# A feed-forward's operand places, its tanh, the splits at the turn, and the loads of the last unit

## The chip, the cores and the metric

The kernel runs on one core of one Trainium2 chip. The metric is the device time of one execution in microseconds, and less is better. Six engines and queues appear below: PE (TensorE, matmuls), PEld (its weight loads), ACT (ScalarE), DVE (VectorE), POOL (GpSimd), and SP (SyncE), which issues the DMAs here.

## What is computed

One encoder layer over 2048 tokens of width 1024, in fp32: windowed attention and a two-way mLSTM beside each other, an output projection, and then the feed-forward, which is the part in question:

```python
hff = rms_norm(x, g_norm2) * (1.0 + scale2) + shift2
gte, up = jnp.split(hff @ w_ffn_in, 2, axis=-1)       # 1024 -> 2 x 2816
ff = (jax.nn.silu(gte) * up) @ w_ffn_out              # 2816 -> 1024
return x + gate2 * ff                                 # then a final rms_norm
```

## The kernel before

Up to about 1000 us the kernel does attention, mLSTM and the output projection; the change touches nothing of it. The rest is the feed-forward, and each of its two products is one level of Strassen and Winograd: seven products of half size in place of eight. The operands are sums and differences of quarters, named A11, A12, S1 to S4, A22 on one side and B11, B21, B22, T1 to T4 and the like on the other. Each operand is split into two parts, hi (a copy that ScalarE rounds) and lo (the rest, by a subtraction on VectorE, line 1370 for the token side, 1405 for the weights, 1666 and 1675 in the down projection). Each product of operands is three matmuls in `mm3` (lines 56, 57, 58: hi by hi, hi by lo, lo by hi).

**Up projection.** `pair(hh, j)` is a unit: one column tile of gate and up for one half of the tokens. It runs seven products (`prod(0)` to `prod(6)`, 12 matmuls of 128x512 each), and between them the evacuations of PSUM: `s1_`, `g0`, a tanh into `t0` (silu is made from it), `u2`, `c5`, `u3`, a second tanh, and so on; these small tiles come from six buffers in turn (`ot`). There are 44 units, numbered from 0: 22 for the first half of the tokens, then 22 for the second in reversed order. Between unit 21 and unit 22 lies the turn: unit 22 uses the weights of unit 21 again, and `refill_ops(1)` loads the second half's seven operands from `hop_d` and splits them (`finish_op`, two halves of 128x1024 for each). Weights for the next unit are loaded (`load_raw`) and split (`weights`) beside the current one. The split weights are the stationary operands of these matmuls, and go through a ring of twelve tiles: four `big`, four `w`, and r0 to r3 in the pool `ff`.

A unit's results are combined on POOL and stored to `a_d` in DRAM. A store is put on a list and issued at the next unit's start (`stores`, line 1539).

**Down projection.** For each of seven operand kinds it runs over 11 k and 8 blocks of rows, 1848 matmuls in all. The stationary operands are `ah` and `al` (`raw_a` loads them from `a_d`, line 1661; `split_a` splits them), which go through the ring `aring` of eight tiles; `w2` goes through `wring`. The first of these loads and splits begin in the last unit of the up projection.

**What sets the order.** The program is written in one sequence; the build reorders it by priority and free buffers, and then each engine works its own queue strictly in order, and so does SP with its DMAs. A tile is written again only when all readers of its last content are done.

**Places.** Before, r0 to r3 are at bytes 204,768 to 221,152 of each partition and the rows `x1t` and the tiles `xt` in the pool `xp`; the other eight tiles of the weights' ring are below 158,720.

Of the kernel before, what the change touches and what calls it, by code (L numbers as in the profile page):

```python
# [11 lines left out]
F32 = mybir.dt.float32  # L12
# [3 lines left out]
AF = mybir.ActivationFunctionType  # L16
ALU = mybir.AluOpType
MUL, ADD, SUB, MAX, MIN = ALU.mult, ALU.add, ALU.subtract, ALU.max, ALU.min
# [3 lines left out]
P = 128  # L22
T = 2048
D = 1024
# [12 lines left out]
def hybrid_layer_kernel(  # L37
# [93 lines left out]
    def big(i, name, shape=(P, 2, 512), dt=F32R):  # L131

        return hp.tile(list(shape), dt, tag=f"big{i}", name=name)
# [112 lines left out]
    with tc.tile_pool(name="sw", bufs=2, side="right", reuse_waits="tile") as sw:  # L246
# [135 lines left out]
        r = rsqrt(s1, ssq, 4, D, "rs")  # L382
# [928 lines left out]

    def norm2(hh, z, tags, lead):
        n = BO[2 * hh + z]
        xt = [xp.tile([P, D], F32, tag="xt", name="x1t", bufs=4) for _ in range(4)]
        for i in range(4):
            sp.dma_start(xt[i], x1_d[(4 * n + i) * P:(4 * n + i + 1) * P, :])
        op = {o: hop_d[hh, i] for i, o in enumerate(OPS)}
        new = lambda: xp.tile([P, 512], F32, tag="n2", name="n2", bufs=5)
        for _ in range(lead):
            yield True  # L1320
        ssq = xp.tile([P, 4], F32, tag="ssq", name="ssq")
        for i in range(4):
            jk = xp.tile([P, D], BF16, tag="junk", name="junk", bufs=1)
            act.activation(jk, xt[i], AF.Square, accum_out=ssq[:, i:i + 1])
            yield True
        r = rsqrt(xp, ssq, 4, D, "rs")
        yield True
        yield True
        for i in range(4):
            act.activation(xt[i], xt[i], AF.Copy, scale=r[:, i:i + 1])  # L1330
            yield True
        if z == 0:
            for k in range(KT):
                t = new()
                turned(t, xt, k, tags[k % 2], gs2, mod[:, 3, :])
                yield True
                sp.dma_start(op["B11" if k < 4 else "B21"][k % 4], t)
        else:
            for k in range(4):
                b11, b21, b12, b22, t3 = (new() for _ in range(5))  # L1340
                sp.dma_start(b11, op["B11"][k])
                sp.dma_start(b21, op["B21"][k])
                turned(b12, xt, k, tags[0], gs2, mod[:, 3, :])
                yield True
                turned(b22, xt, k + 4, tags[1], gs2, mod[:, 3, :])
                yield True
                dve.tensor_tensor(t3, b22, b12, SUB)
                dve.tensor_tensor(b12, b12, b11, SUB)
                dve.tensor_tensor(b11, b22, b12, SUB)
                yield True  # L1350
                dve.tensor_tensor(b21, b21, b11, SUB)
                for o, t in (("B22", b22), ("T3", t3), ("T1", b12), ("T2", b11)):
                    sp.dma_start(op[o][k], t)
                yield True
                sp.dma_start(op["T4"][k], b21)

    def refill_ops(hh):


        hls = []  # L1360

        def start(u):
            hls.append([[big(4 * u + 2 * z + i, OPS[u]) for i in range(2)] for z in range(2)])
            for i in range(2):
                sp.dma_start(hls[u][1][i].bitcast(F32), hop_d[hh, u, 2 * i:2 * i + 2].rearrange("k p t -> p k t"))

        def finish(u):
            for hi, lo in zip(*hls[u]):
                act.activation(hi, lo.bitcast(F32), AF.Copy)
                dve.tensor_tensor(lo, lo.bitcast(F32), hi.bitcast(F32), SUB)  # L1370

        return hls, finish, start

    ring = deque([("big", f"big{i}") for i in range(28, 32)] + [("w", f"w{i}{z}") for i in (1, 0) for z in "hl"]
                 + [("ff", f"r{i}") for i in range(4)])
    pools = {"w": wp, "big": hp}

    def ring_tile(name, shape=(P, 2, 512)):
# [14 lines left out]
        sp.dma_start(v(a22), w_ffn_in[512:1024, cu].rearrange("(k p) c -> p k c", p=P))  # L1393
        return g, a21, a22

    def weights(raw, early=False):

        g, a21, a22 = raw
        a11, a12 = g[:, :512], g[:, 512:]
        ws_ = {}  # L1400

        def part(n, f):
            t = ws_[n] = ring_tile(n)
            act.activation(t[:, 0, :], f, AF.Copy)  # L1404
            dve.tensor_tensor(t[:, 1, :], f, t[:, 0, :].bitcast(F32), SUB)  # L1405

        f1, f2 = (xd.tile([P, 512], F32, tag="n2", name="sf", bufs=9) if early else
                  pools["ff"].tile([P, 512], F32, tag="sf", name="sf", bufs=2) for _ in range(2))
        pool.tensor_tensor(f1, a21, a22, ADD)  # L1409
        pool.tensor_tensor(f2, f1, a11, SUB)  # L1410
        part("A11", a11)
        yield True
        part("A12", a12)
        pool.tensor_tensor(a21, a11, a21, SUB)
        yield True
        pool.tensor_tensor(a12, a12, f2, SUB)
        part("S2", f2)
        yield True
        part("S1", f1)
        yield True  # L1420
        part("S3", a21)
        yield True
        part("S4", a12)
        yield True
        part("A22", a22)
        yield [ws_[n] for n in ("A11", "A12", "S2", "S1", "S3", "S4", "A22")]

    NPR, KH, raws, put_off = NT // 2, DFF // P // 2, [], []
# [97 lines left out]
    with tc.tile_pool(name="ff", bufs=1, side="right", reuse_waits="tile") as ff:  # L1526
# [15 lines left out]
        def pair(hh, j, ws_, hop, after=lambda u: None, then=lambda u: None):  # L1542
# [20 lines left out]
            then(0)  # L1563
            prod(1, ps2, True)
            dve.tensor_tensor(g0, ps2, s1_, ADD)
            act.activation(t0, g0, AF.Tanh, scale=0.5)
            dve.scalar_tensor_tensor(g0, t0, 1.0, g0, ADD, MUL)
            then(1)
            prod(2, ps1)
            act.activation(u2, ps1, AF.Copy)  # L1570
            then(2)
            prod(3, ps5, True)
            act.activation(c5, ps5, AF.Copy)
# [40 lines left out]
        JO = [m * KH + j for j in range(KH) for m in range(2)]  # L1614
        units = [(0, j) for j in JO] + [(1, j) for j in reversed(JO)]
        wseq = deque(JO[2:] + JO[-2::-1])
        raw, = raws
        for n, (hh, j) in enumerate(units[:-1]):
            ws_, turn = nxt_w, n == NJ - 1
            start = lambda u: None  # L1620
            if turn:
                hop1, finish_op, start = refill_ops(1)
                assert not norms
            else:
                more_w = weights(raw)
            STEPS = (0, 0, 0, 2, 2, 1, 2) if n == 0 else (0, 0, 1, 1, 2, 2, 1)

            def beside(u):

                nonlocal nxt_w, raw  # L1630
                if n == 0 and u < 3:
                    finish_op(u + 4)
                if n == NJ and u < 2:
                    finish_op(u + 5)
                if turn:
                    if u > 1:
                        finish_op(u - 2)
                    return
                for _ in range(STEPS[u]):
                    nxt_w = next(more_w)  # L1640
# [7 lines left out]
                hop = hop1  # L1648


        aring = deque([("ff", f"r{i}") for i in range(4)] + [("w", f"w{i}{z}") for i in (1, 0) for z in "hl"])
        wring = deque([("xp", "xt")] * 4)

        def from_ring(rg, name, shape):
            pl, tag = rg[0]
# [159 lines left out]
        def evac(u, i, ps):  # L1815
            if u == "A11":
                ra.append(big(16 + i, "ra", (P, D), F32))
            if u == "S3":
                rb.append(big(24 + i, "rb", (P, D), F32))
            a, b = (t[i] if i < len(t) else None for t in (ra, rb))  # L1820
            if u in ("A11", "S2", "S3", "A22"):
                z, m = {"A11": (a, 0), "S2": (a, 1), "S3": (b, 1), "A22": (b, 0)}[u]
# [18 lines left out]
        for u in ("A11", "S2", "S3", "A22", "S1", "S4", "A12"):  # L1841
# [17 lines left out]
                if u == "S1" and 0 < k <= 8:  # L1859
                    row0(k - 1)  # L1860
            if u == "A12":
                aring.extendleft(("big", f"big{31 - i}") for i in range(8))
            tail = [operands(u, k) for k in range(KH - KL, KH)]
            for i in range(8):
                for k, (a, w) in enumerate(tail):
# [32 lines left out]
```

## Time and profile before

| | |
|---|---|
| median of 3 runs | 2327.73 us (2326.14 to 2330.36) |
| profiled execution, span | 2327.4 us |
| PE busy | 2247.9 us, 97% of the span |
| DVE, ACT, POOL busy | 1579.2, 1060.3, 1047.7 us |
| units 0 to 20 and 23 to 42 | 19.0 to 20.7 us each |
| unit 21, unit 22 (the turn) | 20.8, 31.2 us |
| unit 43 (the last) | 27.0 us |
| first six k of the down projection | 41.1 us |

Rows of windows give, for each stretch, the busy time of each engine with its count, then the TensorE clock that was granted (1.00 is full), the share of time in which the DMA engines were busy, and GB/s. Rows of the timeline give start, length, engine, line, tile written and read, and in brackets how long the engine had stood idle and what ended that. Rows of waits give line waited at, what was waited for, microseconds in all, times, and the longest.

### The profile page before, as it was taken

Reading aid. Unit: us, or ns where it says so; the run is one execution under the profiler, and the core shown is the slowest. Engines: PE = TensorE matmul, PEld = TensorE weight load, DVE = VectorE, ACT = ScalarE, POOL = GpSimd, SP = SyncE. Lnnn points to the kernel's source line nnn. Section 1 sums busy time; section 2 is a strip of 40 time slices with the busy share of each in tenths; the row PEclk is TensorE's granted clock in tenths of the full one; section 3 lists DMA queues with packets and bytes.
Section 4 is the critical chain, followed back from the end, with each engine's and each line's share of the span. In section 5 each row is a group of like instructions: output and inputs, shape, how many; then the busy total and the mean of one; then the engine's idle time right before and its main releaser. Section 6 shows DMA issues by size and latency. Waiting matters only on the chain.

```text
span 2327.4 us, 32438 instructions
## 1 busy us (share of the span) xinstructions
PE 2247.9 (97%) x10822; PEld 1864.0 (80%) x10822; DVE 1579.2 (68%) x2931; ACT 1060.3 (46%) x2206; POOL 1047.7 (45%) x876
## 2 busy tenths in 40 slices
PE   7999999999999999999999999899999989999998
PEld 4997778888788878778888887788788868888887
DVE  6786567656787797786656767666666636684594
ACT  5423555544677655344444434333333323232352
POOL 1006534334334344536565665556565643592020
PEclk9999999999999999999999999999999989999999
DMA  8486755686756667754343545223232373442462
GB/s 329 153 251 211 241 169 158 187 235 173 214 173 190 182 225 244 236 208 145 109 168 104 172 150 217 68 95 109 95 109 95 126 259 104 162 151 99 135 218 91
DMA packets 355499, 393.38 MB, mean 169 GB/s; under 512 B 21388, under 2 KB 253180, under 8 KB 355332
## 3 DMA queue, kind: packets, MB, share of 16 engines
q1 hardware_dynamic: 355108, 391.28, 52.0%
q8 instruction: 85, 1.39, 0.2%
q14 instruction: 82, 0.67, 0.1%
q10 hardware_dynamic: 224, 0.04, 0.0%
HBM read 272.05 MB, written 119.19 MB: 168 GB/s over the span
## 4 chain that ended last, share of the span: by engine, by line
PE 53%; DMA 2%; DVE 2%; issue 1%; ACT 1%; POOL 0%; SPq 0%; ACTq 0%; DVEq 0%; POOLq 0%
PE fp L56 11%; PE fp L57 11%; PE fp L58 11%; PE fo L58 6%; PE fo L57 6%; PE fo L56 6%; DMA a_d<-u 1%; PE ops L56 1%; PE ops L57 1%; PE ops L58 1%; DMA al<-a_d 1%; DVE S L1405 0%; DMA B<-hop_d 0%; PE trn L166 0%; DMA T<-hop_d 0%
## 5 line engine op out<-in xcount | busy, mean ns | idle before, releaser
L466 PE MATMUL gps<-hT,whi 128*128 128x512 f32 x1088 | 398.1, 420 | 0.3 <-DVE cacc L500 0.3
L56 PE MATMUL fo<-w,ah 128*128 128x512 f32 x616 | 242.9, 394 | 2.7 <-DVE u L1589 1.5
L58 PE MATMUL fo<-w,al 128*128 128x512 f32 x616 | 242.6, 394 | 1.4 <-DVE al L1666 1.4
L57 PE MATMUL fo<-w,ah 128*128 128x512 f32 x616 | 242.6, 394 | 0.0
L466 PE MATMUL gps<-hT,wlo 128*128 128x512 f32 x544 | 227.7, 419 | 0.0
L56 PE MATMUL fp<-T,S 128*128 128x512 f32 x528 | 209.3, 396 | 12.0 <-ACT u L1570 11.0
L466 PEld LDWEIGHTS gps<-hT,whi 128*128 128x128 f32 x1088 | 201.1, 191 | 24.5 <-DVE cacc L500 0.7
L57 PE MATMUL fp<-T,S 128*128 128x512 f32 x528 | 207.5, 393 | 0.0
L58 PE MATMUL fp<-T,S 128*128 128x512 f32 x528 | 207.4, 393 | 0.0
L1666 DVE TENSOR_TENSOR al<-al,ah 128x1024 fp32r<-128x1024 f32 x77 | 116.5, 1516 | 124.5 <-ACT ah L1665 124.0
L1405 DVE TENSOR_TENSOR A<-graw,A 128x512 fp32r<-128x512 f32 x86 | 101.6, 1186 | 121.7 <-ACT A L1404 119.3
L1665 ACT ACTIVATE ah<-al 128x1024 fp32r<-128x1024 f32 x77 | 81.5, 1059 | 194.6 <-DMA al<-a_d 190.6
L1405 DVE TENSOR_TENSOR S<-sf,S 128x512 fp32r<-128x512 f32 x86 | 128.8, 1535 | 59.2 <-ACT S L1404 59.2
L56 PEld LDWEIGHTS fo<-w,ah 128*128 128x128 f32 x616 | 116.2, 189 | 30.0 <-DVE u L1589 1.9
L58 PEld LDWEIGHTS fo<-w,al 128*128 128x128 f32 x616 | 116.2, 189 | 28.1 <-DVE al L1666 1.8
L58 PE MATMUL fp<-B,A 128*128 128x512 f32 x352 | 137.6, 391 | 0.0
L56 PE MATMUL fp<-B,A 128*128 128x512 f32 x352 | 137.6, 391 | 0.0
L57 PE MATMUL fp<-B,A 128*128 128x512 f32 x352 | 137.6, 391 | 0.0
L57 PEld LDWEIGHTS fo<-w,ah 128*128 128x128 f32 x616 | 116.2, 189 | 26.4
L756 POOL TENSOR_SCALAR ap<-ap,adn 128x384 f32<-128x384 f32 (+1 forms) x128 | 73.1, 590 | 126.0 <-DVE adn L754 48.8
L56 PEld LDWEIGHTS fp<-T,S 128*128 128x128 f32 x528 | 99.6, 189 | 36.5 <-ACT u L1570 13.1
L1409 POOL TENSOR_TENSOR sf<-A,A22r 128x512 f32<-128x512 f32 x43 | 58.4, 1359 | 151.6 <-DMA A22r<-in_w_ffn_in_dram 111.9
(418 smaller groups left out, 6104.8 us busy)
## 6 DMA issues: line engine op xcount, KB each, us to landing
al<-a_d SPq DMA_DIRECT2D x77, 512.0 KB, 3.6
wmod<-in_w_mod_dram SPq DMA_DIRECT2D x48, 512.0 KB, 6.9
graw<-in_w_ffn_in_dram SPq DMA_DIRECT2D x43, 512.0 KB, 3.9
a_d<-ka SPq DMA_DIRECT2D x66, 256.0 KB, 4.6
bc<-bc_d SPq DMA_DIRECT2D x64, 256.0 KB, 3.6
hop_d<-n SPq DMA_DIRECT2D x56, 256.0 KB, 4.6
a_d<-u SPq DMA_DIRECT2D x55, 256.0 KB, 4.6
mqk<-qk_d SPq DMA_DIRECT2D x48, 256.0 KB, 4.4
```

Of the source, the lines that this page charges most:

```text
L56: pe.matmul(o, lh, rh, start=first, stop=False, skip_group_check=skip)
L57: pe.matmul(o, lh, rl, start=False, stop=False, skip_group_check=skip)
L58: pe.matmul(o, ll, rh, start=False, stop=last, skip_group_check=skip)
L466: pe.matmul(ps, w[i == 2][:, k, :], hT[n](i == 1, k), start=(k == 0 and i == 0), stop=(k == KT - 1 and i == 2))
L756: pool.tensor_scalar(self.p[g][:, :self.NK], self.p[g][:, :self.NK], dn[:, g:g + 1], 0.0, MUL, ADD)
L1405: dve.tensor_tensor(t[:, 1, :], f, t[:, 0, :].bitcast(F32), SUB)
L1409: pool.tensor_tensor(f1, a21, a22, ADD)
L1665: act.activation(ah, al.bitcast(F32), AF.Copy)
L1666: dve.tensor_tensor(al, al.bitcast(F32), ah.bitcast(F32), SUB)
```

## The change

It has four parts. (1) r0 to r3 move to the pool `xp`, where they lie at bytes 158,720 to 175,104; the rows `x1t` and the tiles `xt` move to `ff`, at 212,960 to 229,344. (2) In each unit the tanh into `t0` and what follows it come behind the third product and its `u2` copy. (3) At the turn the splits of the second half's operands are dealt over products 3 to 6 of unit 21 and 0 to 3 of unit 22 by a table, some of them by halves; and beside unit 0 the part A22 of the next weights is split first. (4) In the last unit the first loads for the down projection go into the `w` tiles and later into r0 to r3, `w2` goes through four `big` tiles, and the tiles for the last operand kind are listed anew.

```diff
-        xt = [xp.tile([P, D], F32, tag="xt", name="x1t", bufs=4) for _ in range(4)]
+        xt = [pools["ff"].tile([P, D], F32, tag="xt", name="x1t", bufs=4) for _ in range(4)]
...
-        def finish(u):
-            for hi, lo in zip(*hls[u]):
+        def finish(u, part=slice(None)):
+            for hi, lo in list(zip(*hls[u]))[part]:
...
-                 + [("ff", f"r{i}") for i in range(4)])
+                 + [("xp", f"r{i}") for i in range(4)])
...
+        if last_first:
+            part("A22", a22)
         part("A11", a11)
...
-        part("A22", a22)
+        if not last_first:
+            part("A22", a22)
...
             dve.tensor_tensor(g0, ps2, s1_, ADD)
-            act.activation(t0, g0, AF.Tanh, scale=0.5)
-            dve.scalar_tensor_tensor(g0, t0, 1.0, g0, ADD, MUL)
             then(1)
             prod(2, ps1)
             act.activation(u2, ps1, AF.Copy)
+            act.activation(t0, g0, AF.Tanh, scale=0.5)
+            dve.scalar_tensor_tensor(g0, t0, 1.0, g0, ADD, MUL)
             then(2)
...
+        A, B, BOTH = slice(0, 1), slice(1, 2), slice(0, 2)
+        REFILL = {3: [(0, BOTH)], 4: [(1, BOTH)], 5: [(2, BOTH)], 6: [(3, A)], 7: [(3, B), (4, A)],
+                  8: [(4, B), (5, A)], 9: [(5, B), (6, A)], 10: [(6, B)]}
...
-                more_w = weights(raw)
+                more_w = weights(raw, False, n == 0)
...
-                if n == NJ and u < 2:
-                    finish_op(u + 5)
+                if turn or n == NJ:
+                    for o, part in REFILL.get(u + 7 * (n == NJ), ()):
+                        finish_op(o, part)
                 if turn:
-                    if u > 1:
-                        finish_op(u - 2)
                     return
...
-        aring = deque([("ff", f"r{i}") for i in range(4)] + [("w", f"w{i}{z}") for i in (1, 0) for z in "hl"])
-        wring = deque([("xp", "xt")] * 4)
+        aring = deque([("w", f"w{i}{z}") for i in (1, 0) for z in "hl"] + [("xp", f"r{i}") for i in range(4)])
+        wring = deque([("big", f"big{i}") for i in (29, 30, 31, 28)])
...
-                rb.append(big(24 + i, "rb", (P, D), F32))
+                rb.append(big(24 + i, "rb", (P, D), F32) if i < 4 else
+                          ff.tile([P, D], F32, tag="xt", name="rb", bufs=4))
...
-                aring.extendleft(("big", f"big{31 - i}") for i in range(8))
+                aring.extendleft(("ff", "xt") if i is None else ("big", f"big{i}")
+                                 for i in (None, None, 1, 0, 27, 26, 25, 24))
```

What stands in a row on the engines, in three places of the built program. Numbers behind a name tell one buffer from another.

ScalarE at the turn, in unit 22: splits of the operands B22, T1, T3, T4 (line 1369), and the evacuations s1, t0, u2. Before:

```order
L1562 ACTIVATE s1_15442<-fp_15448 128x512
L1369 ACTIVATE B22_15397<-B22_15399 128x1024
L1369 ACTIVATE B22_15398<-B22_15400 128x1024
L1566 ACTIVATE t0_15444<-g0_15443 128x512
L1369 ACTIVATE T4_15422<-T4_15424 128x1024
L1369 ACTIVATE T4_15423<-T4_15425 128x1024
L1570 ACTIVATE u2_15445<-fp_15448 128x512
```

and after:

```order
L1565 ACTIVATE s1_15436<-fp_15442 128x512
L1369 ACTIVATE T1_15347<-T1_15349 128x1024
L1369 ACTIVATE T3_15369<-T3_15371 128x1024
L1369 ACTIVATE T3_15370<-T3_15372 128x1024
L1369 ACTIVATE B22_15393<-B22_15395 128x1024
L1571 ACTIVATE u2_15439<-fp_15442 128x512
L1572 ACTIVATE t0_15438<-g0_15437 128x512
```

The u2 copy has moved ahead of the tanh and of the T4 splits. VectorE at the same place, where g0 is the addition that the tanh reads, before:

```order
L1370 TENSOR_TENSOR B22_15399<-B22_15399,B22_15397 128x1024
L1370 TENSOR_TENSOR B22_15400<-B22_15400,B22_15398 128x1024
L1565 TENSOR_TENSOR g0_15443<-fp_15449,s1_15442 128x512
L1567 SCALAR_TENSOR_TENSOR g0_15443<-t0_15444,g0_15443 128x512
L1370 TENSOR_TENSOR T4_15424<-T4_15424,T4_15422 128x1024
L1370 TENSOR_TENSOR T4_15425<-T4_15425,T4_15423 128x1024
```

and after:

```order
L1370 TENSOR_TENSOR T3_15371<-T3_15371,T3_15369 128x1024
L1568 TENSOR_TENSOR g0_15437<-fp_15443,s1_15436 128x512
L1370 TENSOR_TENSOR T3_15372<-T3_15372,T3_15370 128x1024
L1370 TENSOR_TENSOR B22_15395<-B22_15395,B22_15393 128x1024
L1573 SCALAR_TENSOR_TENSOR g0_15437<-t0_15438,g0_15437 128x512
L1370 TENSOR_TENSOR B22_15396<-B22_15396,B22_15394 128x1024
L1370 TENSOR_TENSOR T4_15420<-T4_15420,T4_15418 128x1024
L1405 TENSOR_TENSOR A11_15502<-graw_15258,A11_15502 128x512
L1370 TENSOR_TENSOR T4_15421<-T4_15421,T4_15419 128x1024
```

The g0 addition now stands ahead of three splits that were ahead of it. SP in the last unit; al_18525 and al_18543 (after: al_18541) are the loads for k = 0 and 1, the other two those for k = 2 and 3. Before:

```order
L1661 DMA al_18713<-a_d_76 128x1024
L1539 DMA a_d_76<-ka0_18488 128x512
L1539 DMA a_d_76<-ka1_18489 128x512
L1698 DMA w2x_18710<-in_w_ffn_out_dram 128x512 x2
L1698 DMA w2x_18745<-in_w_ffn_out_dram 128x512
L1661 DMA al_18748<-a_d_76 128x1024
L1698 DMA w2x_18745<-in_w_ffn_out_dram 128x512
L1698 DMA w2x_18780<-in_w_ffn_out_dram 128x512 x2
L1698 DMA w2x_18815<-in_w_ffn_out_dram 128x512
L1661 DMA al_18525<-a_d_76 128x1024
L1698 DMA w2x_18815<-in_w_ffn_out_dram 128x512
L1698 DMA w2x_18850<-in_w_ffn_out_dram 128x512 x2
```

and after:

```order
L1542 DMA a_d_76<-ka0_18488 128x512
L1542 DMA a_d_76<-ka1_18489 128x512
L1666 DMA al_18525<-a_d_76 128x1024
L1703 DMA w2x_18710<-in_w_ffn_out_dram 128x512
L1666 DMA al_18541<-a_d_76 128x1024
L1750 DMA g2h_18495<-gate_d_73 128x1024
L1703 DMA w2n_18577<-in_w_ffn_out_dram 128x512
L1703 DMA w2n_18613<-in_w_ffn_out_dram 128x512
L1703 DMA w2x_18745<-in_w_ffn_out_dram 128x512
L1666 DMA al_18713<-a_d_76 128x1024
```

The loads for k = 0 and 1 now stand ahead of those for k = 2 and 3. ScalarE in unit 0, around its `c5` and `u3` copies, before:

```order
L1573 ACTIVATE c5_11954<-fp_11958 128x512
L1404 ACTIVATE A11_12029<-graw_11926 128x512
L1404 ACTIVATE A12_12032<-graw_11926 128x512
L1576 ACTIVATE u3_11955<-fp_11956 128x512
L1404 ACTIVATE S2_12051<-sf_12026 128x512
```

and after:

```order
L1576 ACTIVATE c5_11954<-fp_11958 128x512
L1404 ACTIVATE A22_12029<-A22r_11928 128x512
L1404 ACTIVATE A11_12032<-graw_11926 128x512
L1404 ACTIVATE A12_12035<-graw_11926 128x512
L1579 ACTIVATE u3_11955<-fp_11956 128x512
```

One more copy, A22, stands between c5 and u3.

More of the change, by code (lines that the diff above doesn't have):

```diff
@@ L1394, in load_raw, with weights @@
         return g, a21, a22
-    def weights(raw, early=False):
+    def weights(raw, early=False, last_first=False):
         g, a21, a22 = raw
```

## The prediction

> **What bounds the kernel now.** I read the page's busy times first, then windows over the feed-forward, then TensorE's waits, then the stages in which those fall.
>
> ```profile
> span 2327.4 us, 32438 instructions
> PE 2247.9 (97%) x10822; PEld 1864.0 (80%) x10822; DVE 1579.2 (68%) x2931; ACT 1060.3 (46%) x2206; POOL 1047.7 (45%) x876
> ```
>
> TensorE is busy for 97% of the span. The change adds and removes no matmul, so it can gain in two ways only: TensorE stands or runs slowly less often, or a matmul takes less time. Windows over all engines (TensorE, weight loads, VectorE, ScalarE, GpSimd; then granted clock, DMA share, GB/s) show where it stands:
>
> ```profile
> 1420.00:1473.00 53.00, 42.62 (x174) 33.85 (x173) 37.18 (x33) 24.92 (x35) 22.38 (x12) 0.90 0.52 193
> 1473.00:1858.00 385.00, 383.34 (x1674) 313.58 (x1673) 239.03 (x239) 145.00 (x259) 239.85 (x160) 1.00 0.32 104
> 1858.00:1920.00 62.00, 52.78 (x203) 41.23 (x202) 24.38 (x25) 15.94 (x24) 30.33 (x20) 0.89 0.71 250
> 1920.00:2320.00 400.00, 399.39 (x1737) 325.40 (x1735) 269.82 (x380) 140.28 (x194) 133.54 (x73) 1.00 0.41 137
> ```
>
> Two short places stand out: the turn (10.4 us idle, clock 0.90) and the last unit with what follows (9.2 us idle, 0.89). Elsewhere TensorE is full at clock 1.00 and VectorE has a third of its time free. TensorE's waits in the feed-forward name the causes:
>
> ```profile
> PE fp L56 <- ACT u L1570: 11.0, 5, 8.0
> PE fp L56 <- ACT c L1573: 6.8, 3, 5.1
> PE fo L56 <- DVE u L1589: 1.5, 1, 1.5
> PE fo L58 <- DVE al L1666: 1.4, 1, 1.4
> PE fo L56 <- DVE u L1580: 1.2, 1, 1.2
> ```
>
> **Term 1, the place of the stationary operand.** In a full stage a matmul's pitch is not always the same. The first two rows are TensorE alone in the down projection, 48 matmuls each (a count one higher holds one cut by the edge); the last two are all engines in the up projection, 96 and 48 matmuls.
>
> ```profile
> 1960.50:1971.70 11.20, 11.20 (x49) 1.00 0.32 95
> 1971.70:1982.60 10.90, 10.90 (x50) 1.00 0.31 96
> ...
> 1678.20:1700.00 21.80, 21.80 (x97) 17.97 (x96) 12.99 (x13) 8.31 (x15) 16.19 (x12) 1.00 0.33 109
> 1700.00:1711.20 11.20, 11.20 (x49) 9.00 (x48) 8.44 (x9) 4.43 (x8) 5.92 (x4) 1.00 0.05 13
> ```
>
> The stretches of 11.20 us are those whose stationary operand lies in r0 to r3 of the pool ff, at 200 KB and higher of each partition in the built program; those of 227 ns a matmul (21.80/96, 10.90/48) have it below 155 KB. The difference is 0.30/48 = 6.2 ns. Before, 2112 of the 5544 feed-forward matmuls have it high; after, r0 to r3 lie at 155 to 171 KB, and 24 matmuls stay high (the xt tiles in the down projection). No row shows a 512-wide matmul with its stationary operand at 155 to 171 KB: the ends are as at 155 KB, 2088 x 6.2 = 13.0 us gained, and as at 200 KB, nothing. 155 is the nearer: **-13.0**.
>
> The Trainium skill (SBUF — State Buffer, section "SBUF: two separate sides") says that inside the engines' side only the port pair shared by VectorE and GpSimd causes contention and TensorE never waits on anyone. Read strictly, an operand's place would cost nothing and this term would be zero. The rows above, 227 against 233 ns at full clock with nothing waited for, disagree with that reading for the old place.
>
> **Term 2, the turn.** Unit 22 uses unit 21's weights while seven operands, 14 halves, for the second half of the tokens are split, each half by a ScalarE copy and a VectorE subtraction. An unstalled unit, then units 21 and 22, then what TensorE did after its wait of 8.0 us:
>
> ```profile
> 1711.20:1730.40 19.20, 19.20 (x86) 1.00 0.30 92
> ...
> 1420.60:1441.40 20.80, 19.41 (x85) 1.00 0.81 291
> 1441.40:1472.60 31.20, 22.21 (x85) 0.84 0.35 134
> 1461.70:1467.00 5.30, 5.24 (x12) 0.50 0.00 0
> ```
>
> 52.0 us against 38.4 is 13.6 lost: 10.4 in waits, and 12 matmuls at half clock, 5.3 for 2.7. The cause is a chain over two engines. First ScalarE, then VectorE, then the subtractions from 1434 to 1462.7 and their spread:
>
> ```profile
> 1458.71 0.63 ACT L1566 ACTIVATE t<-g 128x512 f32<-128x512 f32 x1 [8.79 <-DVE g L1565]
> 1461.14 0.57 ACT L1570 ACTIVATE u<-fp 128x512 f32<-128x512 f32 x1
> ...
> 1457.99 0.68 DVE L1565 TENSOR_TENSOR g<-fp,s 128x512 f32<-128x512 f32 x1
> ...
> L1370 DVE TENSOR_TENSOR T<-T,T 128x1024 fp32r<-128x1024 f32 x8 | 14.0, 1784 | 0.7 <-ACT T L1369 0.7
> L1370 DVE TENSOR_TENSOR B<-B,B 128x1024 fp32r<-128x1024 f32 x6 | 9.3, 1576 | 5.9 <-ACT B L1369 5.8
> ...
> L1370 DVE TENSOR_TENSOR T<-T,T x8: 1212/1886/2306, 1439.2 to 1461.5; 128x1024 fp32r<-128x1024 f32 x8
> ```
>
> The u2 copy, for which TensorE waits, stands behind the tanh, the tanh behind the g0 addition, and that behind the splits on VectorE. After, the u2 copy stands ahead of the tanh and the splits are dealt over ten products, so that chain goes. Late next is VectorE itself: 14 subtractions (14.0 + 9.3 = 23.3), six small operations of 0.69 (4.1) and about 1.0 for the copies that start it, from 1434.0: the last split is ready near 1462.4, the seventh product of unit 22 runs behind it for 2.75 and ends near 1465.1, against 1472.6 before: **-7.5**. Ends: with all 14 at 1.21 VectorE is no bound and the whole 13.6 goes; with all at 2.31 (9.0 more) the unit ends 1.5 later than before. I take the measured mean, since GpSimd's work beside it stays.
>
> **Term 3, the last unit and the turn into the down projection.** The last unit, then the first six k of the down projection (144 matmuls, 32.7 us at 227 ns), and the two stretches of half clock:
>
> ```profile
> 1859.40:1886.40 27.00, 21.85 (x85) 0.87 0.76 273
> 1886.40:1927.50 41.10, 37.03 (x146) 0.92 0.65 228
> 1878.50:1883.40 4.90, 4.87 (x12) 0.50 0.54 206
> 1894.40:1900.60 6.20, 6.15 (x15) 0.50 0.28 103
> ```
>
> 68.1 us against 51.9: 16.2 lost. SyncE's queue first, then ScalarE, GpSimd, and SyncE again:
>
> ```profile
> 1870.63 0.33 SPq L1661 DMA_DIRECT2D al<-a_d  x1
> 1871.00 6.37 SPq L1698 DMA_DIRECT2D w2x<-in_w_ffn_out_dram  x9
> 1883.90 0.33 SPq L1661 DMA_DIRECT2D al<-a_d  x1
> ...
> 1876.42 1.06 ACT L1665 ACTIVATE ah<-al 128x1024 fp32r<-128x1024 f32 x1 [2.80 <-DMA al<-a_d]
> ...
> 1905.28 1.73 POOL L1607 TENSOR_TENSOR ka<-ka,g 128x512 f32<-128x512 f32 x1
> ...
> 1907.45 0.38 SPq L1661 DMA_DIRECT2D al<-a_d  x1
> ```
>
> The rows for k=0 and 1 go into r0 to r3, which the last unit still reads; they are loaded at 1870.63 and 1883.90, late, and their ScalarE copies hold up c5 (5.1 us waited, then half clock) and the second tanh (1.2 and 1.5, then 15 matmuls at half clock). The load for k=4 waits until 1907.45 behind the last store of the unit, whose producer on GpSimd is interleaved with preparing w2 (1.4). After, k=0 and 1 go into w tiles which the last unit does not read, their loads stand first on SyncE, and GpSimd's chain stands in one piece: seven operations of 1.3 to 1.7 from about 1880, stores away near 1889, k=4 split near 1895, needed near 1900. So all four waits and both half-clock stretches should go. I leave 1.2 of the 16.2, of which 0.9 is in term 1 already: **-15**. Ends: -9 if the c5 wait alone goes (5.1, its half clock 2.2, and 1.4), -15.3.
>
> **Term 4, three waits for stores.**
>
> ```profile
> 1658.08 0.60 ACT L1570 ACTIVATE u<-fp 128x512 f32<-128x512 f32 x1 [4.69 <-DMA a_d<-u]
> ```
>
> Besides the 8.0 at the turn, TensorE waits four times for L1570, 11.0 - 8.0 = 3.0 together; three of the four (in the units at 1294, 1541 and 1658) are u2 copies like this one, into a buffer whose last content is still being stored. After, that buffer falls to t0, whose tanh no product waits for at once: 3.0 x 3/4, **-2.2**; ends -3.0 and 0.
>
> **Term 5, the first unit pays.** After, the part A22 is split first there, and the place it frees is where A11 is to be written. ScalarE's u3 copy stands behind the A11 and A12 copies, these behind VectorE's A22 subtraction, and this behind the T4 splits:
>
> ```profile
> 1020.28 4.55 DVE L1370 TENSOR_TENSOR T<-T,T 128x1024 fp32r<-128x1024 f32 x2
> ...
> 1021.00 0.58 ACT L1573 ACTIVATE c<-fp 128x512 f32<-128x512 f32 x1
> 1021.48 1.15 ACT L1404 ACTIVATE A<-graw 128x512 fp32r<-128x512 f32 x2
> 1022.52 0.58 ACT L1576 ACTIVATE u<-fp 128x512 f32<-128x512 f32 x1
> ```
>
> T4 ends at 1024.83, the subtraction 0.7 later, two copies 1.15, u3 0.58: 1027.2. TensorE starts the sixth product when c5 is done (1021.6), ends it at 1024.4 and then needs u3, which was there at 1023.1: **+2.8**; ends 0 (if VectorE takes A22 earlier) and +5.4 (a half-clock stretch of 2.6 behind it).
>
> **At nothing:** 64 transposes of the norm whose rows move up to 208 KB (at 6.2 ns, 0.4 at most), the other tiles for w2 and the A12 part: from 1920 to 2320 VectorE is busy for 270 and ScalarE for 140 of 400 us, which covers them. If that cover went, a wait would show at 8 places per operand kind.
>
> **The sum.** -13.0 - 7.5 - 15 - 2.2 + 2.8 = -34.9 against the profiled span of 2327.4, so 2292.5; the median of the runs, 2327.73, is 0.3 above the span: **2293**.
>
> **Rivals.**
> *The place is worth nothing at 155 to 171 KB*, because the step in price lies below 155 and not between 171 and 200. For it: no row covers the stretch. Against: it is nearer to the fast rows. It gives 2293 + 13 = 2306.
> *VectorE binds harder at the turn.* If dealing out the splits puts each of them against a GpSimd operation, they take 2.31 (+9.0), with a half-clock stretch (+2.6): 2302 to 2305. For it: the median of T is 1.89 already. A stretch of half clock followed waits of 8.0 and 5.1 us, and also two waits of 1.2 and 1.5 us inside 3 us, so shorter stalls close together may bring one as well.
> The Trainium skill (TensorE: Matmul & The Clock Gate, "What's actually happening") puts the fall to half clock behind a whole idle window of about 3.4 us. By that rule the spread stalls of the turn and the 2.8 us of term 5 would cost no clock; the pair of short waits here disagrees.
> *The last unit is healed by half*: the DMA share there is 0.76 already, so earlier loads may land late. +7.5: 2300.
> *Slower than before:* the five stores of the last unit wait in SyncE's queue for GpSimd's chain, and k=4 stands behind them. The chain must end later than in the trace (1907.0) by the whole gain, near 1940, for TensorE to stand 35 us. For it only that GpSimd's operation at 1889.66 had waited 9.2 for a w2 load; against it, that the chain no longer stands behind such work. 2330 then.
>
> **How the numbers follow.** Chances: forecast 0.68 (its own range 2285 to 2298, by the ends of terms 2 and 3), place worth nothing 0.08, VectorE at the turn 0.12, last unit by half 0.10, slower 0.02. The range 2284 to 2306 takes in the full gain at the turn and the first two rivals each alone. What a measurement here can tell from no change is 0.2%, 4.7 us: two terms lost together still leave more than that, so faster 0.97, same 0.01, slower 0.02.
>
> **What the profile after would show.** Term 1: every stretch of 48 matmuls in 10.9 us, 2088 x 6.2 ns less matmul time in the feed-forward. Term 2: the wait on the u2 copy at the turn gone, units 21 and 22 in about 44 us, short waits for VectorE's T subtractions in unit 22. Term 3: the last unit in 19 to 20 us, no clock of 0.5 behind 1858, al for k=4 loaded before 1895. Term 4: no waits on the u2 copy at 1294, 1541 and 1658. Term 5: a new wait of 2 to 3 us for u3 near 1024. The forecast is wrong if matmuls keep 11.2 us per 48, or if units 22 or 43 still take over 24 us.

## The result, and the profile after

The changed kernel takes 2293.1 us (median, 2290.8 to 2293.6); the kernel before took 2329.05 beside it. The ratio is 0.9852, with a 95% interval of 0.9837 to 0.9867. The forecast was 2293. The profiled execution took 2290.8 us, 2.1 more than its span.

The page after, its first and busy lines:

```profile
span 2288.7 us, 32479 instructions
PE 2226.4 (97%) x10822; PEld 1860.2 (81%) x10822; DVE 1607.5 (70%) x2931; ACT 1059.1 (46%) x2206; POOL 1060.1 (46%) x876
```

TensorE is busy 21.5 us less with the same 10822 matmuls, and the span is 38.7 shorter: more than half of the gain is matmuls that take less time or run at full clock, the rest is idle time. TensorE's waits from 940 us on, those of the feed-forward:

```profile
PE fp L57 <- DVE T L1370: 2.7, 4, 0.9
PE fp L56 <- ACT c L1576: 2.1, 2, 1.6
PE fp L56 <- ACT u L1579: 1.7, 1, 1.7
```

All waits of the down projection are gone, and no wait is over 1.7 us, where there was one of 8.0. What is left lies at the turn (the T splits, and 0.6 for c5) and in unit 0 (1.6 for c5, 1.7 for u3). TensorE alone in unit 0, units 21 and 22, unit 43, and the 144 matmuls behind it:

```profile
1006.10:1029.00 22.90, 19.64 (x86) 1.00 0.55 185
...
1417.80:1436.80 19.00, 19.00 (x85) 1.00 0.79 285
1436.80:1461.30 24.50, 21.15 (x85) 1.00 0.51 197
1842.10:1861.20 19.10, 19.10 (x86) 1.00 0.90 307
1861.20:1893.80 32.60, 32.60 (x145) 1.00 0.87 322
```

Unit 21 and unit 43 are as short as any, the clock is 1.00 in every row, and unit 22 went from 31.2 to 24.5; only unit 0 got longer. By the starts of the matmuls, a stop costs TensorE 0.2 to 0.3 us beyond its idle time, even at full clock: unit 0 has two stops, 3.3 us idle together, and takes 3.9 more than a unit without any (19.04). A look at one full stretch of the down projection, 264 matmuls, first before and then after:

```profile
2015.90:2076.60 60.70, 60.70 (x266) 1.00 0.56 186
```

```profile
2041.00:2100.80 59.80, 59.80 (x265) 1.00 0.31 97
```

By the matmuls' starts, from the feed-forward's first to its last, the gain is 38.2 us: the up projection's full units together 10.5, the turn 8.5, the last unit with the 144 matmuls behind it 16.4, the rest of the down projection 4.9, unit 0 -2.2 (lost). The 36.0 of the medians is of other executions than the two profiled ones, whose spans differ by 38.7. Where those 2 us lie is not shown, but the part ahead of the feed-forward, which the change does not touch, varies by more: the feed-forward's first matmul came between 1004.9 and 1014.8 us in the eleven profiles of the layer, and single runs of the kernel before took from 2324.9 to 2337.1. So what follows reads the stages and the whole time only beside them. A stage without waits repeats to 0.1 us: the rest of the down projection took 391.50 before and 391.53 and 391.50 in two kernels whose edits leave it alone (a third, with a wait of 0.3 in it, 392.3). One with waits does not: the last unit took 27.1 before and 25.7 with a change at the turn alone. Each kernel was profiled once.

### The profile page after: what moved, and what is told of

It is laid out like the page before. It is cut to its first block, busy times and chain, and to the rows that moved or that the text cites. A ratio compares the mean times of both kernels' runs of the same rounds, so it can differ in the third digit from the quotient of the medians.

```text
span 2288.7 us, 32479 instructions
## 1 busy us (share of the span) xinstructions
PE 2226.4 (97%) x10822; PEld 1860.2 (81%) x10822; DVE 1607.5 (70%) x2931; ACT 1059.1 (46%) x2206; POOL 1060.1 (46%) x876
## 4 chain that ended last, share of the span: by engine, by line
PE 55%; DVE 1%; issue 1%; DMA 1%; ACT 0%; POOL 0%; SPq 0%; DVEq 0%; POOLq 0%; ACTq 0%
PE fp L57 12%; PE fp L56 12%; PE fp L58 12%; PE fo L56 6%; PE fo L57 6%; PE fo L58 6%; PE ops L56 1%; PE ops L57 1%; PE ops L58 1%; DVE T L1370 0%; PE trn L166 0%; DMA B<-hop_d 0%; DMA A22r<-in_w_ffn_in_dram 0%; DVE B L1370 0%; DVE xr L1176 0%
## 5 line engine op out<-in xcount | busy, mean ns | idle before, releaser
L57 PE MATMUL fo<-w,ah 128*128 128x512 f32 x616 | 239.7, 389 | 0.0
L56 PE MATMUL fo<-w,ah 128*128 128x512 f32 x616 | 239.7, 389 | 0.0
L1405 DVE TENSOR_TENSOR A<-graw,A 128x512 fp32r<-128x512 f32 x86 | 127.2, 1501 | 17.0 <-ACT A L1404 17.0
L1573 DVE SCALAR_TENSOR_TENSOR g<-t,g 128x512 f32<-128x512 f32 x44 | 44.4, 1009 | 133.4 <-ACT t L1572 133.4
```

The source lines that it names most:

```text
L56: pe.matmul(o, lh, rh, start=first, stop=False, skip_group_check=skip)
L57: pe.matmul(o, lh, rl, start=False, stop=False, skip_group_check=skip)
```

## The experiments

### Part 1 alone

```diff
-    xt = [xp.tile(... "x1t" ...)]           # and A22 first in unit 0
+    xt = [pools["ff"].tile(... "x1t" ...)]
-    ring: ... ("ff", f"r{i}")      aring: ("ff", r)   wring: ("xp", "xt")
+    ring: ... ("xp", f"r{i}")      aring: ("xp", r)   wring: ("ff", "xt")
```

> Part 1 alone: r0 to r3 low, the xt tiles high, A22 split first in unit 0; the rings keep their order, so the down projection's w2, which is the streamed (moving) operand, now lies at 213 KB in 1728 of its 1848 matmuls. Theory (only the stationary operand's place costs): units of the up projection 7.6 us less in all (1224 x 6.2 ns), unit 0 about 2.5 more, the down projection 10.9 us per 48 matmuls, 5.5 less; in all -10.5, 2317. Rival (any operand at 200 KB or more costs): the down projection 11.2 us per 48 nearly everywhere, 5.2 more than before; in all about 0, 2328. The turn (52 us for units 21 and 22) and the last unit (27) stay in both.

Measured: ratio 1.0013 (1.0000 to 1.0027). The units 23 to 42 took 382.3 us for 386.7 and a plain unit 19.04, as the theory has it. But the down projection went the other way:

```profile
2018.80:2080.30 61.50, 61.50 (x265) 1.00 0.56 184
...
L57 PE MATMUL fo<-w,ah 128*128 128x512 f32 x400 | 158.2, 395 | 0.0
```

264 matmuls took 61.5 for 60.7, all of them at the slow pitch, though now the stationary operand is low and the streamed one, w2, is in `ff`. The rival holds: either operand brings the price. Unit 0 took 25.4, which is 4.7 more than before where 2.5 were expected: TensorE waited 2.6 for u3, with a stretch of half clock behind it. Part 1 alone is worth nothing; it needs part 4, which takes w2 out of `ff`.

### Part 2 alone, the dealing alone, and both

```diff
-            act.activation(t0, g0, AF.Tanh, scale=0.5)        # ahead of prod(2)
             prod(2, ps1)
             act.activation(u2, ps1, AF.Copy)
+            act.activation(t0, g0, AF.Tanh, scale=0.5)        # tanh order
...
-                if n == NJ and u < 2: finish_op(u + 5)        # dealing
+                if turn or n == NJ:
+                    for o, part in REFILL.get(u + 7 * (n == NJ), ()):
```

> Part 2 alone: u2 copy ahead of the tanh. Theory: the three store waits go (-2.2); at the turn the u2 copy no longer stands behind the T4 splits, but the fourth product then waits for the B22 splits, which ended at 1458.1, so 3 to 6 us of 13.6 are gained there; in all about -7, 2321, the last unit still 27. Rival (the turn is the dealing's alone): only -2.2, 2326, a wait of 8 us still in unit 22.

> The dealing of the splits over ten products alone, with the tanh still ahead of the u2 copy. Theory (VectorE's work is the bound once the g0 addition is not behind all splits): units 21 and 22 together 45 to 48 us for 52, no wait over 3 us, in all -4 to -7, 2322. Rival (the tanh ahead of u2 is what hurts): units 21 and 22 still 50 or more, in all within 2 us of before.

> Parts 2 and 3 (the dealing) together, without the others. Alone, units 21 and 22 took 47.4 (tanh order) and 46.8 (dealing) for 52.1. Theory (each takes a piece of the same wait, and VectorE with the loads is what is left): about 43.9, as in the whole change but for 0.3 of place. Rival (the two gains add): 42.1. The last unit stays at about 26, the next 144 matmuls at about 42.

Measured: the tanh order 0.9978 (0.9967 to 0.9989), the dealing 0.9981 (0.9969 to 0.9994); the third ran once, with a profile. TensorE in units 21 and 22, in this order of kernels:

```profile
1420.30:1441.30 21.00, 19.41 (x85) 1.00 0.81 293
1441.30:1467.70 26.40, 21.37 (x86) 0.94 0.41 155
```

```profile
1425.10:1444.30 19.20, 19.20 (x86) 1.00 0.80 287
1444.30:1471.90 27.60, 22.59 (x85) 0.88 0.44 171
```

```profile
1424.70:1443.90 19.20, 19.20 (x86) 1.00 0.80 285
1443.90:1468.10 24.20, 20.91 (x85) 1.00 0.51 197
```

Each alone gains 4.7 and 5.2 us and leaves a wait of 4.0 (for c5) or 4.4 (for u2) with a stretch of half clock behind it (0.94, 0.88). Neither was the wait expected: with the tanh order the fourth product did not wait for the B22 splits, but the c5 copy stood behind the tanh and so behind the same g0 addition, and with the dealing a wait of over 3 us stayed. Together they gain 8.6, not 9.9, and the half clock is gone; their theory holds. The tanh order also took the store waits away: units 14, 26 and 32 took 58.3 us for 61.1. In all it gained 4.5 of the 7 expected, mainly since unit 0 grew from 20.7 to 23.1, of which term 5 below has the cause. In the third kernel unit 0 took 23.2, and the 144 matmuls behind the last unit 39.6 where 42 were expected, since no half clock came there this time.

### Part 4 alone

```diff
-        aring = deque([("ff", f"r{i}") for i in range(4)] + [("w", ...)])
-        wring = deque([("xp", "xt")] * 4)
+        aring = deque([("w", ...)] + [("ff", f"r{i}") for i in range(4)])
+        wring = deque([("big", f"big{i}") for i in (29, 30, 31, 28)])
...                                       # and the last operand kind's tiles, as in the change
```

> Part 4 alone: first loads of the down projection into the w tiles, w2 into big tiles. Theory: the last unit 19 to 20 us for 27, the next 144 matmuls about 33 to 34 for 41, no half clock there; -15, 2313; turn unchanged at 52. Rival (the last unit needs the new tanh order as well): half of it, -7, with a wait on the u2 or c5 copy left in the last unit.

Measured: ratio 0.9929 (0.9912 to 0.9946), 2312.1 us.

```profile
1441.20:1472.00 30.80, 21.81 (x85) 0.83 0.36 138
1858.30:1877.60 19.30, 19.30 (x85) 1.00 0.92 325
1877.60:1910.60 33.00, 33.00 (x146) 1.00 0.82 301
```

The last unit and the 144 matmuls went from 68.1 to 52.3 us, 15.8 less, with no wait and no half clock, while the turn stayed at 30.8. The theory holds; no other part is needed there.

### The change without part 1

```diff
# the changed kernel, with r0 to r3 in ff, xt in xp, and unit 0's splits as before
```

> The changed kernel without part 1: r0 to r3 high again, the xt tiles low, unit 0's splits in the old order; 2088 more matmuls have their stationary operand at 200 KB. Theory (place is a term of its own): +13.0 by 6.2 ns each, and unit 0 back to about 20.7 to 21.5 (-1.5 to -2.2): 2293 + 11 = 2304. Rival (the place saves only in full stages, waits eat it elsewhere): under +7, 2300 or less.

Measured: 2304.0 us. TensorE in its unit 0:

```profile
1006.70:1028.10 21.40, 19.40 (x86) 1.00 0.57 196
```

By the feed-forward's own time it takes 11.8 us more than the change: 13.3 more in the stages other than unit 0 (7.2 in the full units, 5.7 in the down projection, the rest at the turn and in the last unit), and 1.6 less in unit 0 (21.4 for 22.9). So part 1 is worth 13.3 in those stages, against 13.0 forecast. Its size was right.

### What about the place costs

```diff
+    for k in STAT: 96 matmuls, stationary at k KB, streamed at 64 KB
+    for k in MOVE: 96 matmuls, stationary at 8 KB, streamed at k KB
```

> None of the layer: on one core, 96 matmuls of 128x512 for each of 20 places of the stationary operand (names s008k to s216k, KB in a partition, 1 KB above; the streamed operand at 65 KB), then for each of 11 places of the streamed operand (m008k to m216k, the stationary one at 9 KB), then both high. Theory: one step in price, between 172 and 200 KB, the same for both operands: mean of one matmul 389 ns below and 395 above, 21.8 and 22.4 us for 96; with both high 395 still, since the down projection of the first experiment, with one of them high in each matmul, took 11.2 us per 48 throughout. Rival 1: the price grows in proportion with the place. Rival 2: it adds for both operands, 401 ns.

Neither theory nor rivals held. The rows below are the 96 matmuls with the stationary operand at 217 KB, with the streamed one at 209, and with both high:

```profile
L63 PE MATMUL s216k<-W 128*128 128x512 f32 x96 | 21.9, 389 | 0.0
L63 PE MATMUL m208k<-W 128*128 128x512 f32 x96 | 21.9, 389 | 0.0
L63 PE MATMUL bothk<-W 128*128 128x512 f32 x96 | 21.9, 389 | 0.0
```

There is no step: the pitch was 226.7 ns at all places (a pause of TensorE falls into each of the first three groups and is left out of it). So here the place as such costs nothing, and what was slow in the layer must differ in something else. In the built program every slow operand starts 96 bytes past a multiple of 128 (204,768 is one), because the right-hand pools grow downward from byte 229,344; every fast one starts at a multiple of 128, as do all operands of this experiment. Low operands were all of the one kind and high ones all of the other, so place and remainder cannot be told apart in the kernel before.

### Shifting the pool by 32 bytes

```diff
+    gap = ctx.enter_context(tc.tile_pool(name="gap", side="right", ...))
+    dve.memset(gap.tile([P, 8], F32, tag="gap", name="gap", bufs=1), 0.0)
     with tc.tile_pool(name="ff", bufs=1, side="right", ...) as ff:
```

> The kernel before with 32 bytes reserved above the pool ff, and nothing else: all 2112 matmuls keep their stationary operand at 200 KB or more, but it now starts at a multiple of 64 bytes, where before it started 32 bytes off. New theory (the start's remainder by 64 is what costs, not the place): 10.9 us per 48 throughout, 13 us less, 2315; waits as before (unit 22 31 us, the last unit 27). Old theory (the place): no change, 2328.

Measured: 2319.5 us, ratio 0.9956 (0.9940 to 0.9972). The two rows are 48 matmuls each of the down projection, the first with the stationary operand low, the second with it above 200 KB and now 64 bytes past a multiple of 128:

```profile
1962.50:1973.40 10.90, 10.90 (x49) 1.00 0.31 96
1973.40:1984.40 11.00, 11.00 (x49) 1.00 0.33 97
```

With nothing moved but by 32 bytes, 11.2 became 11.0. The old theory is refuted. The new one was two thirds right: the pitch fell from 233.3 to 229.0 ns, not to 226.7, so a multiple of 64 bytes is not enough. For 2112 matmuls that makes 9.1 us, and the medians differ by 9.1.

### Offsets by themselves

```diff
+    a = s * KB + so // 4 + 128 * (i % 8)      # stationary start, so bytes off
+    b = m * KB + mo // 4 + 512 * (i % 2)      # streamed start, mo bytes off
```

> None of the layer: 96 matmuls each with the stationary operand 0, 4, 8, 16, 32, 48, 64, 96 bytes off a 64-byte grid at 9 KB (s00low to s96low) and five of these at 209 KB (s00high to s64high), then the streamed operand (m00low to m96low at 65 KB, m32high, m64high at 201 KB), then both off by 16 and by 32. New theory: 0 and 64 bytes 21.8 us for 96 at every place; 32 and 96 22.4 us, for either operand; both off no more than one. Open: 4 to 16 and 48, which may cost the same as 32 or half. Rival (something else of the layer, such as the other engines' accesses, is needed beside the offset): 21.8 throughout.

```profile
L62 PE MATMUL s00high<-W 128*128 128x512 f32 x96 | 21.9, 389 | 0.0
L62 PE MATMUL s32high<-W 128*128 128x512 f32 x96 | 22.6, 395 | 0.0
L62 PE MATMUL s64low<-W 128*128 128x512 f32 x96 | 22.6, 395 | 0.0
L62 PE MATMUL m32low<-W 128*128 128x512 f32 x96 | 22.6, 395 | 0.0
L62 PE MATMUL m64low<-W 128*128 128x512 f32 x96 | 22.1, 391 | 0.0
L62 PE MATMUL m04low<-W 128*128 128x512 f32 x96 | 22.9, 399 | 0.0
L62 PE MATMUL both32low<-W 128*128 128x512 f32 x96 | 21.9, 389 | 0.0
```

Here too 64 bytes off is slow and a multiple of 128 fast, at a low and at a high place, for either operand, with no other engine at work. An offset of 32 costs 6.6 ns on either side, and 96, the layer's, 6.7 (streamed) and 7.6 (stationary). Two rows were not expected: both operands off by 32 cost nothing, and the stationary one off by 16 at the high place cost nothing either (21.9), while at the low place it cost 6.6. An offset of 64 of the stationary operand cost 6.6 here and 2.3 in the layer. So it is shown that starts at multiples of 128 were fast without exception and that a start 32 bytes off on one side was slow; a rule for the offsets between is not shown, and in the layer itself a high place at a multiple of 128 was not run. That both off alike are fast speaks for the two starts counting against each other, but this was not tried further.

### Short idle times and the clock

```diff
+    for n in range(8): a train of 72 to 87 matmuls, then n + 2 ScalarE copies in a chain
+    then pairs of short idle times with 6, 12 or 24 matmuls between
```

> None of the layer: trains of 72 to 87 matmuls with idle times between them in which ScalarE does 2 to 9 copies (names longaw to longhw, each four times), then pairs of short idle times with 6, 12 or 24 matmuls between. Theory (a short idle time alone costs no clock, a long one always does, with a limit between 1.7 us, after which the clock stayed full in the changed kernel, and 5.1 us, after which it was halved in the kernel before; between, it depends on the moment): no half clock after idle times to about 2 us, always from about 5 us, some of the four in between; pairs with 6 matmuls between them are halved in some of four. Rival (the clock looks only at the longest single idle time): pairs never.

The waits that the profile shows at the next train, in microseconds in all, times, longest:

```profile
PE longfw L58 <- ACT W L65: 16.2, 4, 4.1
PE longew L58 <- ACT W L65: 13.6, 4, 3.4
PE longdw L58 <- ACT W L65: 10.9, 4, 2.7
PE longcw L58 <- ACT W L65: 8.3, 4, 2.1
PE longbw L58 <- ACT W L65: 5.9, 4, 1.7
PE pair06s L58 <- ACT W L65: 5.6, 4, 1.4
```

By the pitch of the matmuls behind them, waits of 1.4 to 1.7 never halved the clock, 2.1 did once in four, 2.7 three times in four, 3.4 and more always. Two windows of 3 us behind waits of 2.1, and one behind 3.4:

```profile
66.80:69.80 3.00, 2.98 (x13) 1.00 0.00 0
243.60:246.60 3.00, 2.98 (x8) 0.55 0.00 0
...
107.80:110.80 3.00, 3.00 (x7) 0.50 0.00 0
```

So the same wait can cost nothing or 7 to 14 slow matmuls: between 1.7 and 3.4 us these runs do not show what decides. The layer's unit 0 agrees: behind waits of 2.2, 2.5 and 2.6 in three kernels the clock was halved, behind one of 2.0 it was not. The prediction weighed whether a wait of 2.8 us would cost no clock; three of the four waits of 2.7 here did cost it. The pairs never halved it, in twelve tries, so the rival held for them. The pair in the kernel before that did, with waits of 1.2 and 1.5, had only three matmuls between (3.7 us from the start of the first wait to the end of the second, not 3 as the prediction has it), where the pairs here have at least six. The layer's other traces have it too: waits of 1.1 to 1.2 and of 1.4 with three matmuls between stand behind the last unit in the five kernels without part 4, and half clock followed in one of the five. That one, with 32 bytes above the pool, comes first here, and then a kernel where it did not follow, the tanh order with the dealing:

```profile
1886.30:1889.30 3.00, 2.97 (x7) 0.50 0.36 134
```

```profile
1886.70:1889.70 3.00, 3.00 (x13) 1.00 0.32 121
```

So the same pair, too, can cost the half clock or nothing, two times in six with the kernel before; what decides stays open.

### Two versions beyond the change

```diff
# first (shortened): unit 0, the turn's loads, and 32 bytes above all right-hand pools
-                if n == 0 and u < 3: finish_op(u + 4)
+                if n == 0 and u in (0, 1, 3): finish_op(u + 4 - u // 3)
+        if last_first: part("A22", a22); yield True          # A11 comes behind u3
+        stores() and load_raw() of the turn behind the hop_d loads
# second: the same with r0 to r3 left in ff and unit 0's split order left
```

> The changed kernel with three more edits: in unit 0 the T4 splits come behind c5 and the u3 copy ahead of A11; at the turn the loads of the second half's operands stand ahead of the stores and of the next weights' loads; 32 bytes are reserved above all pools on the right side, so that the earlier stages' operands there start at multiples of 64. Theory: unit 0 from 22.9 to about 20 (-2 to -3), unit 22 from 24.5 to about 20 (-3 to -5, since the loads ran at 405 GB/s from 1426 to 1448 and set when the splits start), 144 matmuls of the output projection 0.9 less, the rest of the earlier stages 0 to -3: 2286, between 2283 and 2289. Rival (at the turn VectorE beside GpSimd is the bound, not the loads): unit 22 stays over 23, in all 2290.

> As the run before it, but without part 1: r0 to r3 stay at 200 KB, now at multiples of 64 bytes, and unit 0's splits keep their order (T4 behind c5). New theory: part 1's gain is the grid's alone, so this takes within 2 us of the run before it, about 2285. Old theory: 13 us more, 2298.

The first took 2288.0 us, ratio 0.9817 (0.9801 to 0.9834), against 0.9852 of the change: the fastest here. TensorE in its units 0, 21 and 22:

```profile
1014.80:1033.90 19.10, 19.10 (x86) 1.00 0.64 220
1422.70:1441.80 19.10, 19.10 (x86) 1.00 0.87 295
1441.80:1466.20 24.40, 21.09 (x86) 1.00 0.52 189
```

Unit 0 lost all of its waits (19.1 for 22.9), more than expected, and that is the whole gain of its feed-forward over the change's (3.8). Unit 22 did not move, so the rival held there: the first loads were issued 1.3 us after unit 21 began, not 6.1, and still VectorE's first split came 12.7 us after it, as in the change, since its ScalarE copy stands behind c5 by the table. From there VectorE worked with hardly a break. Whether an earlier table would help was not tried.

The second took 2295.6, ratio 0.9847 (0.9829 to 0.9865), 7.6 more by the medians, and its feed-forward 5.1 us more than the first one's. That misses the expectation of 2 and refutes the 13 of the old theory. Of the 5.1, 1.1 is a stop in unit 1, and 4.0 are spread over the other stages: with r0 to r3 64 bytes past a multiple of 128, 2088 matmuls at the 2.3 ns of the shifted pool would make 4.8.

## Why the prediction was right, and where not

**Term 1** (forecast -13.0, measured -13.3 as the price of leaving part 1 out): the size was right and the cause was not. The step that failed is "155 is the nearer": it took the place in the partition for what decides. In its place the runs show the start's remainder by 128 bytes; r0 to r3 moved to 158,720, which is such a multiple, so the forecast hit. By the matmuls alone, a place 32 bytes off and just as low would have gained nothing: there the low place was as slow as the high one (22.6 us for 96 both). That the new place was a multiple of 128 was luck, since the prediction did not look at it. Also, only the stationary operand was counted; w2 would have brought the price back had part 4 not moved it. The rival that the place is worth nothing was right on the place, and still the wrong time. The sentence that the rows disagree with the Trainium skill (SBUF — State Buffer, "SBUF: two separate sides"), which has TensorE wait on no one, does not stand: at all places alike the pitch was 226.7 ns, and what cost was the start of the operand, of which that section says nothing.

**Term 2** (-7.5, measured -8.5, of which 0.2 is term 1's): right in mechanism. VectorE after, at the turn:

```profile
1430.46 2.50 DVE L1370 TENSOR_TENSOR B<-B,B 128x1024 fp32r<-128x1024 f32 x2 [2.47 <-ACT B L1369]
...
1443.66 6.17 DVE L1370 TENSOR_TENSOR T<-T,T 128x1024 fp32r<-128x1024 f32 x3
1449.76 0.68 DVE L1568 TENSOR_TENSOR g<-fp,s 128x512 f32<-128x512 f32 x1
...
1458.79 1.21 DVE L1370 TENSOR_TENSOR T<-T,T 128x1024 fp32r<-128x1024 f32 x1
```

The splits run from 1430.46 to 1460.0, 29.5 us for 28.4 forecast, three in a row at 2.06 each beside GpSimd. What was mis-sized is the tail: the seventh product does not run behind the last split but only its second half does (unit 22 ends 1.3 behind it, not 2.75), and the waits fell in the middle, four of at most 0.9 for T and one of 0.6 for c5. None reached 1.7, and no half clock came, as in the waits experiment.

**Term 3** (-15, measured -16.4, without term 1's share 15.8): every step held. The load for k=4 was issued here:

```profile
1871.28 0.32 SPq L1542 DMA_DIRECT2D a_d<-ka  x1
...
1872.17 0.40 SPq L1666 DMA_DIRECT2D al<-a_d  x1
```

The last store of the unit left at 1871.3, 29.2 us after the unit's start, where the forecast had it at 1889 - 1859.4 = 29.6. The 1.2 us left as a reserve were not needed. The rivals of a half-healed last unit and of a blocked SyncE queue both fall by these rows: the DMA share was 0.90, and TensorE did not wait.

**Term 4** (-2.2, measured -2.8 in the tanh order alone): right. The three waits were 2.2 of idle time, as forecast; the rest is the 0.2 to 0.3 us that each stop costs beside it.

**Term 5** (+2.8, measured +2.2): right in mechanism, with one wait left out. The wait for u3 came, of 1.7 and not 2.8: u3 was there 0.7 us sooner in the unit than forecast and TensorE got to it 0.4 later. VectorE's T4 splits took 4.06 for 4.55 and A22's subtraction followed at once; u3 was there at 1026.1:

```profile
1023.67 0.68 DVE L1405 TENSOR_TENSOR A<-A22r,A 128x512 fp32r<-128x512 f32 x1
```

```profile
1024.43 1.15 ACT L1404 ACTIVATE A<-graw 128x512 fp32r<-128x512 f32 x2 [2.54 <-issue]
1025.48 0.58 ACT L1579 ACTIVATE u<-fp 128x512 f32<-128x512 f32 x1
```

What the step left out: c5's copy, too, stood behind the T4 copies, which wait for a load. In the kernel before TensorE had lost 0.8 us on u2 and 0.25 on c5 there; after, u2 came in time and c5 cost 1.6. The landing had hardly moved (the last T4 copy began 13.6 us into the unit before and 13.7 after), so what the earlier u2 copy saved, the c5 copy lost again. This comes from part 2 and not from A22: the wait on c5 is there in the kernels with the tanh order and A22's old place, here that order alone:

```profile
1020.89 0.50 PE L56 MATMUL fp<-B,S 128*128 128x512 f32 x1 [2.18 <-ACT c L1573]
```

Half clock followed and unit 0 took 23.1 us; in the change without part 1 the same wait was 2.0, no half clock followed, and unit 0 took 21.4. The change's own waits of 1.6 and 1.7 stayed below these, and the forecast's end of +5.4 with half clock was near: part 1 alone came to +4.7. In the version above, which lets c5 pass, both waits are gone.

**The sum** came to -34.9; the stages gave -38.2 and the medians -36.0. The errors of the terms, each without another's share, were -0.3, -0.8, -0.8, -0.6 and -0.6, all the same way. That the median fell on 2293 to a tenth is luck: the medians' gain was 1.1 more than the sum, and the kernel before ran 1.3 slower beside it than the time from which the forecast set out.

## What to carry to other kernels

When two groups of matmuls differ by a steady few nanoseconds at full clock, list every attribute of their operands, the remainder of the start address among them, before choosing one: 32 bytes reserved at the end of a pool gave 9 of the 13 us that moving the tiles gave. An engine's copy that frees a PSUM bank should stand ahead of whatever waits for another engine or a load; of two such waits in a chain, removing one gains about half until the other goes too, and where the chain ends at a load's landing it gains nothing. Read each edit of a change in its own stage: a stage without waits is steady to 0.1 us where the whole time is not to 3, but one with waits can differ by 1 or 2 us between profiles.

## What the runs showed of the hardware that was not expected

- A 128x512 matmul's pitch is 226.7 ns when both operands start at multiples of 128 bytes, and 233.3 ns when one of them starts 32 bytes off, at a low place as at 200 KB and above; 96 off: 233.3 in the layer, 233.4 and 234.3 with matmuls alone. The stationary one 64 off: 229.0 in the layer, 233.3 with matmuls alone. Both off by 32: 226.7.
- TensorE's clock after waits of 2.1 us was halved in one of four cases and after 2.7 in three of four; the halved stretch lasted 7 to 14 matmuls for waits from 2.1 to 6.0 us, without growing with them.
- Two waits of 1.2 and 1.4 us with three matmuls between them halved the clock in two of six kernels and cost no clock in the others.
- A stop of TensorE cost 0.2 to 0.3 us beyond its idle time even where the clock stayed full.
- Loads issued 4.8 us earlier at the turn moved nothing, though before that the profile gave a DMA share of 1.05 there for 20 us: the order on ScalarE set the start.
